# Scan by pairs of chunks, one root per group applied at the turn, taps spread over products, weights split before the seam

## The chip, the cores and the metric

The kernel runs on one core of a Trainium2 chip. The metric is device time in microseconds (us) from start to end of one launch. The kernel before takes 2141.73 us, the median of three runs (2140.22 to 2143.49).

The core has engines with a queue each, worked off in order: TensorE (PE, matrix products), VectorE (DVE), ScalarE (ACT, functions such as exp and silu, whose tables are loaded by an instruction ACT_TABLE_LOAD), GpSimd (POOL) and SyncE (SP), which issues most transfers (DMA). SBUF is the on-chip memory, PSUM the banks into which TensorE writes. Engines wait for each other by semaphores.

## The reference

One block of a streaming encoder on x of 1024 frames by 1024 channels, float32. Cut to what the change touches:

```python
proj = rms_norm(x, norm1_g) @ w_in
lru_x, lru_gate, z, xbc, dt_raw, gates = _split(proj, IN_WIDTHS)
...
xbc = silu(causal_dw_conv(xbc, ssd_conv_w, ssd_conv_b))     # 4 taps
xs, Bm, Cm = _split(xbc, ...)                               # 2048, 512, 512 columns
# scan, per chunk and head:
a_cs = cumsum(dt * A)
decay = exp(where(causal, a_cs[l] - a_cs[s], -inf))
y_diag = (C B^T * decay) @ xdt
states = B^T (decay_to_end * xdt);  h = h * chunk_decay + states
y = y_diag + (C h_prev) * exp(a_cs) + D * xs
# gated norm per group of 512 columns:
y = y * silu(z)
yg = yg * rsqrt(mean(yg * yg) + EPS) * ssd_norm_g
...
merged = g_a * (y_a @ w_branch[:LRU]) + g_b * (y_b @ w_branch[LRU:])
h = x + merged @ w_out
h = h + swiglu(rms_norm(h, norm2_g))
```

There are 32 heads of 64 columns in 4 groups; y_a is the output of another branch, the LRU, a convolution and a linear recurrence.

## The kernel before, in words

Products of float32 matrices are made of two parts: a tile is split (split, L82 and L83) into a high part, cast by ScalarE, and a low part, src minus high, by VectorE; a product takes three matmuls (high by high, high by low, low by high).

The stages, by the time in which they run:

- 0 to 97 us: the first norm, then products of half the gate columns (g_first, g_second, L308). Beside them row_sums makes, in two halves of two row blocks, sums and differences of the normalised x (f00 to f11) and splits them into t1 to t4 (L386, L387).
- 90 to 455 us, the units: 20 units of 256 columns each, 12 for xbc and 8 for the gates. A unit is made of 7 products (5 for the gates) over quarter matrices, so that sums of quarters stand on one side (unit_sums, GpSimd) and t1 to t4 on the other; useq lists the products. unit_prepare splits a weight part (wc) three products ahead, unit_after takes results out. conv_rows makes the convolution of a finished xbc row block: ScalarE the last tap with the bias (L432), VectorE three taps (L435), ScalarE the silu (L437), SP the transfer.
- 455 to 463 us, the seam: t1 to t4 and the units' tiles are given back, the LRU's memory is taken, its first weight is split into w_hi and w_lo.
- 463 to about 682 us: the LRU branch (L659 on). The steps dt and the sums acs of the scan are made in it.
- about 695 to 1075 us, the scan: 4 groups of 8 chunks of 128 frames (the kernel's chunk has twice the reference's length). Per chunk gate_z makes the product of z (24 matmuls, L145) two chunks ahead and its silu sz. chunk_in loads acs, broadcast over 128 partitions, as ed (L733), GpSimd cuts it to the triangle (L735), ScalarE takes 8 exponentials with the bias -acs (L738), one per head; VectorE multiplies it with B C (L762). chunk_out makes the output of the state (py, L775), the new state's product (pst, L779) and the 8 products of ed (pd, L782). VectorE and GpSimd add and gate them (L798 to L803), ScalarE squares with a sum (L807). After every second chunk VectorE makes two columns of reciprocal roots in 12 operations (rsqrt_dve), ScalarE scales both y by them (L812) and SP writes y to memory.
- 1075 to about 1357 us: the branch products over w_branch. add_v reads y back, TensorE turns it (transpose), ScalarE and VectorE split it with the norm's gain. Four of the 16 tiles of y are read at the end of the scan.
- then the merge, w_out, the second norm and the feed-forward layer.

The order within an engine's queue is made by the framework's scheduler out of the code's order and the dependencies; it may put a later independent instruction ahead of a waiting one. A tile named with bufs=n has n buffers in turn. Weights are loaded ahead by load_next and split by split_next.

## Time and profile before

| | us |
|---|---|
| median of three runs | 2141.73 |
| the profiled execution, its own time | 2142.65 |
| its span (first to last instruction) | 2140.8 |
| TensorE busy | 2018.7 (94%) |
| VectorE busy | 1282.9 (60%) |
| ScalarE busy | 965.2 (45%) |
| GpSimd busy | 697.0 (33%) |

Times in the rows are counted from the span's start. The mean granted clock of TensorE is 0.967 of 2.4 GHz. In a row "idle before, releaser" is time in which the engine had nothing to do before the instruction, and what ended it; "issue" is a wait for nothing that the profile shows. An engine's busy time is not its work at full speed: a TensorE at half clock is busy twice as long for the same matmuls.

### The profile page before, as it was taken

To read this page: it belongs to the slowest core of one execution; us is meant where nothing else is said; L and a number is where in the kernel's file an instruction comes from. 1 tells how busy PE (TensorE), PEld (TensorE's weight loads), DVE (VectorE), ACT (ScalarE), POOL (GpSimd) and SP (SyncE) were. 2 spreads that over 40 slices of the span, in tenths; PEclk is the share of its full clock that TensorE was granted. 3 is DMA by queue.
4 is the path that set the end of the run, shared out by engine and by line. 5 is a ranking of instruction groups with operands and counts; after the bars stand their busy time and mean duration, and the time that the engine had idled before them with its cause. 6 is when DMAs were issued, how large, how long until landed. Compare 5 with 4: busy or idle time off the path is not lost.

```text
span 2140.8 us, 23980 instructions
## 1 busy us (share of the span) xinstructions
PE 2018.7 (94%) x8972; PEld 1636.9 (76%) x8972; DVE 1282.9 (60%) x1695; ACT 965.2 (45%) x1545; POOL 697.0 (33%) x472
## 2 busy tenths in 40 slices
PE   6899999989999998898799999998999999999998
PEld 4677777768787786777578788886888888888887
DVE  7887777755575566566624555558554545446445
ACT  5455455447777677677532211335232323242112
POOL 4644444410000667676500011016333233203000
PEclk9999999999999999999599999999999999999999
DMA  5443344332112543432333334531323222256212
GB/s 185 122 123 99 99 127 140 109 102 61 60 54 94 185 143 98 138 99 79 98 99 104 120 119 145 185 104 40 109 69 99 79 69 89 79 176 196 90 60 79
DMA packets 201560, 231.59 MB, mean 108 GB/s; under 512 B 11148, under 2 KB 154980, under 8 KB 201444
## 3 DMA queue, kind: packets, MB, share of 16 engines
q1 hardware_dynamic: 201444, 230.06, 33.7%
q8 instruction: 71, 1.16, 0.2%
q14 instruction: 45, 0.37, 0.1%
HBM read 174.32 MB, written 55.71 MB: 107 GB/s over the span
## 4 chain that ended last, share of the span: by engine, by line
PE 48%; DVE 1%; ACT 1%; issue 0%; ACTq 0%; DVEq 0%
PE mm L308 19%; PE mm L134 13%; PE mm L145 10%; PE aux L145 6%; PE turn L705 1%; PE aux L206 0%; DVE slot L1092 0%; ACT slot L1091 0%; DVE o L1256 0%; DVE xb L1077 0%; DVE xr L1061 0%; DVE t L1081 0%; DVE wc L83 0%; DVE rs_t L163 0%; DVE xb L1083 0%
## 5 line engine op out<-in xcount | busy, mean ns | idle before, releaser
L308 PE MATMUL mm<-slot,wc 128*128 128x512 f32 x2376 | 564.5, 396 | 14.8 <-DVE wc L83 8.2
L308 PEld LDWEIGHTS mm<-slot,wc 128*128 128x128 f32 x2376 | 447.7, 189 | 124.1 <-DVE wc L83 10.6
L134 PE MATMUL mm<-slot,w_hi 128*128 128x512 f32 x768 | 243.6, 398 | 8.7 <-ACT w_hi L82 8.7
L308 PE MATMUL mm<-t,wc 128*128 128x512 f32 x960 | 228.2, 394 | 11.8 <-ACT wc L82 7.1
L145 PE MATMUL mm<-wz,slot 128*128 128x512 f32 x768 | 208.2, 418 | 17.3 <-ACT sz L725 12.9
L308 PEld LDWEIGHTS mm<-t,wc 128*128 128x128 f32 x960 | 181.7, 190 | 53.4 <-ACT wc L82 14.6
L145 PE MATMUL mm<-slot,slot 128*128 128x512 f32 (+1 forms) x924 | 213.0, 387 | 0.0
L145 PEld LDWEIGHTS mm<-slot,slot 128*128 128x128 f32 x924 | 171.6, 188 | 35.0
L145 PEld LDWEIGHTS mm<-wz,slot 128*128 128x128 f32 x768 | 149.0, 200 | 53.6 <-ACT sz L725 16.6
L134 PEld LDWEIGHTS mm<-slot,w_hi 128*128 128x128 f32 x768 | 145.9, 190 | 43.6 <-ACT w_hi L82 9.2
L83 DVE TENSOR_TENSOR wc<-s,wc 128x512 fp32r<-128x512 f32 x168 | 156.1, 952 | 32.6 <-ACT wc L82 32.5
L134 PE MATMUL mm<-slot,w_lo 128*128 128x512 f32 x384 | 151.5, 396 | 0.0
L145 PE MATMUL aux<-slot,slot 128*128 128x512 f32 x528 | 124.4, 389 | 0.0
L435 DVE SCALAR_TENSOR_TENSOR conv<-rows,par,conv 128x1023 f32<-128x1023 f32 (+2 forms) x72 | 111.0, 1541 | 17.3 <-ACT conv L432 17.3
L145 PEld LDWEIGHTS aux<-slot,slot 128*128 128x128 f32 x528 | 99.1, 188 | 20.6
L1028 POOL TENSOR_TENSOR u_u<-u_u,e 128x512 f32<-128x512 f32 x22 | 28.7, 1305 | 261.6 <-DVE u_u L1022 261.6
L82 ACT CAST wc<-s 128x512 fp32r<-128x512 f32 x168 | 98.5, 618 | 16.6 <-DVE wc L83 7.7
L82 ACT CAST slot<-w_raw 128x1024 fp32r<-128x1024 f32 x42 | 43.9, 1051 | 129.4 <-PE mm L145 48.1
L82 ACT CAST w_hi<-w_raw 128x1024 fp32r<-128x1024 f32 x40 | 41.6, 1046 | 118.0 <-PE mm L134 107.2
L907 POOL TENSOR_TENSOR acc<-acc,gt 128x1024 f32<-128x1024 f32 x8 | 20.0, 2512 | 213.3 <-DMA gt<-g_dram 212.2
L134 PE MATMUL mm<-v_even,w_hi 128*128 128x512 f32 x256 | 84.4, 408 | 1.5 <-ACT w_hi L82 1.5
L83 DVE TENSOR_TENSOR slot<-w_raw,slot 128x1024 fp32r<-128x1024 f32 x42 | 53.6, 1281 | 53.4 <-ACT slot L82 53.3
(276 smaller groups left out, 3494.9 us busy)
## 6 DMA issues: line engine op xcount, KB each, us to landing
w_raw<-in_w_in_dram SPq DMA_DIRECT2D x60, 512.0 KB, 3.9
ed<-acs_dram SPq DMA_DIRECT2D x32, 512.0 KB, 3.6
xbc_dram<-conv SPq DMA_DIRECT2D x24, 512.0 KB, 2.7
w_raw<-in_w_branch_dram SPq DMA_DIRECT2D x24, 512.0 KB, 3.4
w_raw<-in_w_ffn_in_dram SPq DMA_DIRECT2D x22, 512.0 KB, 3.9
raw_pair<-in_w_ffn_in_dram SPq DMA_DIRECT2D x22, 512.0 KB, 4.1
act_dram<-act SPq DMA_DIRECT2D x22, 512.0 KB, 2.7
act_raw<-act_dram SPq DMA_DIRECT2D x22, 512.0 KB, 3.5
```

The source lines that it names most:

```text
L82: nc.scalar.copy(out=hi, in_=src)
L83: nc.vector.tensor_tensor(out=lo, in0=src, in1=f32(hi), op=ALU.subtract)
L134: nc.tensor.matmul(ps[:m, :], ww[:, k, :], xx(p, k, h), start=(k == 0 and i == 0), stop=(k == nk - 1 and i == 2))
L145: nc.tensor.matmul(ps, xx(p, k), ww(q, k), start=(k == 0 and i == 0), stop=(k == nk - 1 and i == 2))
L308: nc.tensor.matmul(ps, w[:, k, :], x[q][:, k, :], start=(start and k == 0 and i == 0), stop=(k == 3 and i == 2), skip_group_check=True)
L435: nc.vector.scalar_tensor_tensor(out=t[:, d:], in0=x[:, :S - d], scalar=tap[j], in1=t[:, d:], op0=ALU.mult, op1=ALU.add)
L705: nc.tensor.transpose(out=pt[:, i * P:(i + 1) * P], in_=raw[:, o:o + P], identity=ident)
L907: nc.gpsimd.tensor_tensor(out=acc[m], in0=acc[m], in1=gate_in(1, m), op=ALU.mult)
L1028: nc.gpsimd.tensor_tensor(out=d["u3"], in0=d["u3"], in1=d["e5"], op=ALU.add)
```

## The change

Four parts:

1. Row sums start one product earlier each, and t3 and t4 are split together at the end; the four tiles are taken in the reverse order.
2. conv_rows emits only its second tap at once; the third and the fourth with silu and transfer are put in a list, from which one is taken after each following product.
3. At the last unit product t1 to t4 are given back at once, and the next stage's first weight is split there in the pool of wz (w_early), a second one right after that unit.
4. In the scan ed is made by chunk_ed: load, a subtraction of acs on VectorE, the triangle cut with fill -1e4; the exponential is one of 128x1024. The code loads two chunks' ed and takes two silus and two exponentials one after the other. y is written to memory unscaled; the sums of squares stay in ss_g, and the roots of a group's 8 chunks are made in one go, on 8 columns, and kept in rs_all, by which add_v multiplies y when it is read back, ahead of the turn. ed has 3 buffers for 2, sz 4 for 3, xd 3 for 4, xs2 and xs3 1 for 2.

```diff
-    for name in ("t1", "t2", "t3", "t4"):
+    for name in ("t4", "t3", "t2", "t1"):
         xc[name] = [tq_pool.tile([P, 4, 512], F32R, name=f"{name}_{q}") for q in range(2)]
+
+    def row_parts(name, k, src):
+        ks = slice(k, k + 2)
+        hi = xc[name][0][:, ks]
+        nc.scalar.copy(out=hi, in_=src)
+        nc.vector.tensor_tensor(out=xc[name][1][:, ks], in0=src, in1=f32(hi), op=ALU.subtract)
...
-        for kh in range(2):
-            for h in range(2):
+        for h in range(2):
+            for kh in range(2):
                 f[kh, h] = ubuf(f"f{kh}{h}", [P, 2, 512])
                 (nc.vector if kh == 0 else nc.gpsimd).tensor_tensor(
                     out=f[kh, h], in0=f32(xq[0][kh][h][:, ks]), in1=f32(xq[1][kh][h][:, ks]), op=ALU.add)
         f11, f12, f21, f22 = f[0, 0], f[0, 1], f[1, 0], f[1, 1]
...
         nc.vector.tensor_tensor(out=f11, in0=f12, in1=f11, op=ALU.subtract)
-        parts("t1", f11)
+        row_parts("t1", k, f11)
         nc.gpsimd.tensor_tensor(out=f12, in0=f22, in1=f12, op=ALU.subtract)
         nc.vector.tensor_tensor(out=f22, in0=f22, in1=f11, op=ALU.subtract)
-        parts("t2", f22)
+        row_parts("t2", k, f22)
         nc.gpsimd.tensor_tensor(out=f21, in0=f21, in1=f22, op=ALU.subtract)
-        parts("t3", f12)
-        parts("t4", f21)
+        return f12, f21
...
         g_second(m - 1, gb_[m - 1])
-        if m == 4:
-            row_sums(0)
-        elif m == 6:
-            row_sums(2)
+        if m == 3:
+            t34_0 = row_sums(0)
+        elif m == 5:
+            t34_2 = row_sums(2)
+        elif m == 7:
+            row_parts("t3", 0, t34_0[0])
+            row_parts("t3", 2, t34_2[0])
+            row_parts("t4", 0, t34_0[1])
+            row_parts("t4", 2, t34_2[1])
...
-        for j in (2, 1, 0):
+
+        def one_tap(j):
             d = 3 - j
             nc.vector.scalar_tensor_tensor(out=t[:, d:], in0=x[:, :S - d], scalar=tap[j], in1=t[:, d:],
                                            op0=ALU.mult, op1=ALU.add)
-        nc.scalar.activation(out=t, in_=t, func=AF.Silu)
-        nc.sync.dma_start(out=xbc_dram[tile_no // 2][(tile_no % 2) * P:(tile_no % 2 + 1) * P, :], in_=t)
+
+        def last():
+            one_tap(0)
+            nc.scalar.activation(out=t, in_=t, func=AF.Silu)
+            nc.sync.dma_start(out=xbc_dram[tile_no // 2][(tile_no % 2) * P:(tile_no % 2 + 1) * P, :], in_=t)
+
+        one_tap(2)
+        later.extend([lambda: one_tap(1), last])
+
+    later = deque()
...
+    def w_early():
+
+        raw, _ = loaded.popleft()
+        t = keep_pool.tile([P, 2, KT, P], F32R, name="w_early", tag="wz", bufs=4)
+        split(t[:, 0], t[:, 1], raw)
+        ready.append((t[:, 0], t[:, 1]))
+        load_next()
...
         product(banks[n, HOME[p]], w[:, 0], w[:, 1], xc[XOF[p]], HOME[p] == p)
+        if later:
+            later.popleft()()
+        if i == len(useq) - 1:
+            while later:
+                later.popleft()()
+            t_stack.close()
+            keep_pool = keep_stack.enter_context(phase("keep_pool"))
+            w_early()
         unit_after(n, p)
-    t_stack.close()
+    w_early()
     u_stack.close()
...
-    nacs_t = const.tile([P, NC, NH], F32, name="nacs_t")
+    rs_all = const.tile([P, NG, NC], F32, name="rs_all")
     dec_t = const.tile([P, NC, NH], F32, name="dec_t")
     eacs_t = const.tile([P, NC, NH], F32, name="eacs_t")
     d_bc = const.tile([P, NH], F32, name="d_bc")
-
-    keep_stack = ExitStack()
-    keep_pool = keep_stack.enter_context(phase("keep_pool"))
     sel_last = keep_pool.tile([P, P], F32, name="sel_last")
...
-        nc.vector.tensor_scalar(out=nacs_t, in0=acs_t, scalar1=-1.0, scalar2=None, op0=ALU.mult)
...
+                by_chunk = raw.rearrange("p (c d) -> p c d", d=P)
+                nc.vector.tensor_tensor(out=by_chunk, in0=by_chunk, in1=bcast(rs_all[:, g], P), op=ALU.mult)
...
-            sz = pp.tile([P, GC], F32, name="sz", tag="sz", bufs=3)
+            return zp
+
+        def silu(zp):
+            sz = pp.tile([P, GC], F32, name="sz", tag="sz", bufs=4)
             nc.scalar.activation(out=sz, in_=zp, func=AF.Silu)
             return sz
...
-        def chunk_in(g, c, b_ch, c_ch, xs_ch):
+        def chunk_ed(g, c):
+            hs = slice(g * HG, (g + 1) * HG)
+            ed = pp.tile([P, HG, P], F32, name="ed", tag="ed", bufs=3)
+            nc.sync.dma_start(out=ed, in_=acs_dram[c, hs, :].unsqueeze(0).broadcast_to([P, HG, P]))
+            nc.vector.tensor_tensor(out=ed, in0=ed, in1=bcast(acs_t[:, c, hs], P), op=ALU.subtract)
+
+            nc.gpsimd.affine_select(out=ed, in_=ed, pattern=[[0, HG], [1, P]], compare_op=ALU.is_ge,
+                                    fill=-1.0e4, base=0, channel_multiplier=-1)
+            return ed
+
+        def chunk_in(g, c, b_ch, c_ch, xs_ch, ed):
             h0 = g * HG
             hs = slice(h0, h0 + HG)
             cs = slice(c * P, (c + 1) * P)
-            ed = pp.tile([P, HG, P], F32, name="ed", tag="ed", bufs=2)
-            nc.sync.dma_start(out=ed, in_=acs_dram[c, hs, :].unsqueeze(0).broadcast_to([P, HG, P]))
-
-            nc.gpsimd.affine_select(out=ed, in_=ed, pattern=[[0, HG], [1, P]], compare_op=ALU.is_ge,
-                                    fill=-1.0e30, base=0, channel_multiplier=-1)
-            for h in range(HG):
-                nc.scalar.activation(out=ed[:, h, :], in_=ed[:, h, :], func=AF.Exp, bias=nacs_t[:, c, h0 + h:h0 + h + 1])
             pt = bank()
             nc.tensor.matmul(pt[:, :P], b_ch[:, cs], c_ch[:, cs], start=True, stop=True)
             if c < NC - 1:
@@ -757,12 +793,12 @@
                 xw = pp.tile([P, 2, GC], F32R, name="xw", tag="xw", bufs=1)
                 nc.scalar.copy(out=xw[:, 0, :], in_=flat(xwf))
                 nc.gpsimd.tensor_tensor(out=xw[:, 1, :], in0=flat(xwf), in1=f32(xw[:, 0, :]), op=ALU.subtract)
-            xd = pp.tile([P, HG, 64], F32, name="xd", tag="xd", bufs=4)
+            xd = pp.tile([P, HG, 64], F32, name="xd", tag="xd", bufs=3)
             nc.vector.tensor_tensor(out=xd, in0=pxv, in1=bcast(d_bc[:, hs], 64), op=ALU.mult)
             nc.vector.tensor_tensor(out=ed, in0=ed, in1=pt[:, :P].unsqueeze(1).broadcast_to([P, HG, P]), op=ALU.mult)
             return ed, xdt, xw, xd, b_tm
...
+        ss_g = pp.tile([P, NG, NC], F32, name="ss_g")
...
             nc.gpsimd.tensor_tensor(out=yf, in0=yf, in1=sz, op=ALU.mult)
-            if not pend:
-                ss2[0] = pp.tile([P, 2], F32, name="ss2", tag="ss2", bufs=2)
-            n = len(pend)
-            nc.scalar.activation(out=sz, in_=yf, func=AF.Square, accum_out=ss2[0][:, n:n + 1])
-            pend.append((c, yf))
-            if n:
-                r = rsqrt_dve(pp, ss2[0], 1.0 / GC, 2)
-                for i, (cc, y) in enumerate(pend):
-                    nc.scalar.activation(out=y, in_=y, func=AF.Copy, scale=r[:, i:i + 1])
-                    nc.sync.dma_start(out=y_dram[g][:, :, cc * P:(cc + 1) * P], in_=y.rearrange("p (a b) -> p a b", b=P))
-                pend.clear()
+            nc.scalar.activation(out=sz, in_=yf, func=AF.Square, accum_out=ss_g[:, g, c:c + 1])
+            nc.sync.dma_start(out=y_dram[g][:, :, cs], in_=yf.rearrange("p (a b) -> p a b", b=P))
+            if c == NC - 1:
+                nc.vector.tensor_copy(out=rs_all[:, g, :], in_=rsqrt_dve(pp, ss_g[:, g, :], 1.0 / GC, NC))
             return state
...
+        xs_ch = [rows_of(i, f"xs{i}", 2 if i < 2 else 1) for i in range(4)]
...
-                szs += [gate_z(0, 0), gate_z(0, 1)]
+                eds = [chunk_ed(0, 0), chunk_ed(0, 1)]
+                for e in eds:
+                    nc.scalar.activation(out=e, in_=e, func=AF.Exp)
+                zs = [gate_z(0, 0), gate_z(0, 1)]
+                szs += [silu(z) for z in zs]
+                zs = []
             for c in range(NC):
-                parts = chunk_in(g, c, b_ch, c_ch, xs_ch)
-                if c + 2 < NC:
-                    szs.append(gate_z(g, c + 2))
-                elif g + 1 < NG:
+                parts = chunk_in(g, c, b_ch, c_ch, xs_ch, eds.pop(0))
+                ahead = (g, c + 2) if c + 2 < NC else (g + 1, c + 2 - NC)
+                if ahead[0] < NG:
                     if c + 2 == NC:
                         wz_next(4)
-                    szs.append(gate_z(g + 1, c + 2 - NC))
+                    zs.append(gate_z(*ahead))
+                if c % 2 and ahead[0] < NG:
+                    eds.append(chunk_ed(*ahead))
+                    szs += [silu(z) for z in zs]
+                    zs = []
+                    for e in eds:
+                        nc.scalar.activation(out=e, in_=e, func=AF.Exp)
                 state = chunk_out(g, c, c_hl, parts, state, szs.pop(0))
+                if c % 2 == 0 and ahead[0] < NG:
+                    eds.append(chunk_ed(*ahead))
                 if g == NG - 1 and c >= NC - 2:
                     wz_next(2)
...
-                        xs_next = ([] if c == 3 else xs_next) + [rows_of(4 * g + 1 + c, f"xs{c - 3}", 2)]
+                        xs_next = ([] if c == 3 else xs_next) + [rows_of(4 * g + 1 + c, f"xs{c - 3}", 2 if c < 5 else 1)]
```

In the scheduled program the units have the same instructions in the same order on all engines as before, from the first wc of VectorE on. At the front, VectorE has the low part of the gate weight g_lo for m = 3 behind the first sums, and the second half's part of t2 ahead of the first wc, where it stood behind it. GpSimd's work in the scan is the same.

**ScalarE at the seam.** Before; the first row is the sigmoid of the last gate unit's first rows, neg_a belongs to the scan's steps:

```order
L343 ACTIVATE rows_3240<-rows_3240,par_135 128x512
L475 ACTIVATE rows_3241<-rows_3241,par_135 128x1024
L578 ACT_TABLE_LOAD
L578 ACTIVATE neg_a<-prm 32x1
L82 CAST w_hi<-w_raw 128x1024 x2
L192 ACTIVATE scr<-scr 128x8
```

and now:

```order
L343 ACTIVATE rows_3236<-rows_3236,par_135 128x512
L82 CAST w_early<-w_raw 128x1024 x2
L488 ACTIVATE rows_3237<-rows_3237,par_135 128x1024
L607 ACT_TABLE_LOAD
L607 ACTIVATE neg_a<-prm 32x1
L82 CAST w_hi<-w_raw 128x1024
L561 ACTIVATE u<-mm,par_135 128x512
```

The casts of the first two weights (w_early is called twice) stand ahead of the second sigmoid, in tiles of their own; the weights after them are cast one by one.

**ScalarE in the scan,** two chunks in the middle of the first group, before:

```order
L807 ACTIVATE sz,ss_5354<-xd 128x512
L725 ACT_TABLE_LOAD
L725 ACTIVATE sz<-mm 128x512
L738 ACT_TABLE_LOAD
L738 ACTIVATE ed<-ed,nacs_t 128x128 x8
L812 ACTIVATE xd<-xd,rs_r 128x512 x2
L793 CAST state_hl<-state 128x512
L807 ACTIVATE sz,ss_5577<-xd 128x512
L725 ACT_TABLE_LOAD
L725 ACTIVATE sz<-mm 128x512
L738 ACT_TABLE_LOAD
L738 ACTIVATE ed<-ed,nacs_t 128x128 x8
```

and now (L758 is the silu, L879 the exponential, L840 the square):

```order
L840 ACTIVATE sz,ss_g<-xd 128x512
L758 ACT_TABLE_LOAD
L758 ACTIVATE sz<-mm 128x512
L879 ACT_TABLE_LOAD
L879 ACTIVATE ed<-ed 128x1024
L829 CAST state_hl<-state 128x512
L840 ACTIVATE sz,ss_g<-xd 128x512
L758 ACT_TABLE_LOAD
L758 ACTIVATE sz<-mm 128x512
L879 ACT_TABLE_LOAD
L879 ACTIVATE ed<-ed 128x1024
```

The scaling of two y is gone and the exponential is one instruction; silu and exponential take turns as before, each with its table load, so that there are 28 + 27 + 1 loads (silus, exponentials, the first exponentials) in the scan's lines where there were 25 + 25.

**VectorE in the scan,** a chunk before, with the root of two chunks behind it (of its nine Newton operations, three times the same three, the first three are shown):

```order
L801 TENSOR_TENSOR xd<-aux,xd 128x512
L791 TENSOR_TENSOR state<-aux,state 128x512
L752 TENSOR_TENSOR xdt<-turn,dt_t 128x512
L761 TENSOR_TENSOR xd<-turn,d_bc 128x512
L211 TENSOR_TENSOR b_tm<-aux,b_tm 128x128
L762 TENSOR_TENSOR ed<-ed,aux 128x1024
L170 TENSOR_SCALAR rs_v<-ss_5354 128x2
L172 TENSOR_SCALAR rs_i<-rs_v 128x2
L174 TENSOR_SCALAR rs_r<-rs_i 128x2
L163 TENSOR_TENSOR rs_t<-rs_r 128x2
L164 SCALAR_TENSOR_TENSOR rs_t<-rs_t,rs_v 128x2
L165 SCALAR_TENSOR_TENSOR rs_r<-rs_t,rs_r 128x2
```

and a chunk now:

```order
L827 TENSOR_TENSOR state<-aux,state 128x512
L837 TENSOR_TENSOR xd<-aux,xd 128x512
L788 TENSOR_TENSOR xdt<-turn,dt_t 128x512
L797 TENSOR_TENSOR xd<-turn,d_bc 128x512
L211 TENSOR_TENSOR b_tm<-aux,b_tm 128x128
L798 TENSOR_TENSOR ed<-ed,aux 128x1024
L765 TENSOR_TENSOR ed<-ed,acs_t 128x1024
L834 TENSOR_TENSOR yo<-aux,eacs_t 128x512
```

The root is gone from here. The subtraction (L765), for the chunk three further on, stands last, ahead of the next chunk's yo (L834).

## Rows read from the trace of the kernel before

**Rows 1.** busy time by stretch: us, then PE, PEld, DVE, ACT, POOL, PEclk, DMA share, GB/s

```profile
722.00:1004.50 282.50, 253.81 (x1297) 208.27 (x1296) 188.05 (x325) 203.76 (x420) 194.71 (x156) 0.94 0.36 116
1004.50:1075.00 70.50, 48.82 (x188) 37.98 (x185) 43.30 (x89) 43.38 (x94) 41.87 (x36) 0.57 0.29 90
1075.00:1460.00 385.00, 384.04 (x1726) 311.88 (x1726) 189.88 (x248) 107.61 (x154) 35.48 (x22) 0.99 0.38 125
```

**Rows 2.** TensorE's waits, 60 to 490 us: total us, times, longest

```profile
PE mm L134 <- ACT w_hi L82: 8.7, 1, 8.7
PE mm L308 <- DVE wc L83: 8.2, 5, 6.7
...
PE mm L308 <- DVE rows L455: 4.8, 2, 3.4
```

**Rows 3.** TensorE's waits in the scan, 722 to 1075 us

```profile
PE mm L145 <- ACT sz L725: 12.9, 11, 2.4
PE aux L775 <- ACT state_hl L793: 9.5, 8, 2.8
```

**Rows 4.** line L801: count, duration ns min/median/max, first and last start in us

```profile
L801 DVE TENSOR_TENSOR xd<-aux,xd x32: 676/684/693, 716.9 to 1063.9; 128x512 f32<-128x512 f32 x32
```

**Rows 5.** VectorE's timeline, chunk 24 of the scan: start, us, instruction, idle before

```profile
985.65 0.69 DVE L801 TENSOR_TENSOR xd<-aux,xd 128x512 f32<-128x512 f32 x1
```

**Rows 6.** busy time, 59 to 97 us, columns as in rows 1

```profile
59.00:97.00 38.00, 27.77 (x106) 21.71 (x105) 38.00 (x20) 15.98 (x23) 29.19 (x12) 0.87 0.42 125
```

**Rows 7.** VectorE's timeline at the end of that stretch

```profile
86.95 2.82 DVE L83 TENSOR_TENSOR wc<-w_raw,wc 128x512 fp32r<-128x512 f32 x1
89.70 4.53 DVE L387 TENSOR_TENSOR t<-f,t 128x1024 fp32r<-128x1024 f32 x2
```

**Rows 8.** ScalarE's timeline at the seam: start, us, instruction, idle before

```profile
453.26 0.72 ACT L343 ACTIVATE rows<-rows,par 128x512 f32<-128x512 f32 x1
455.48 1.15 ACT L475 ACTIVATE rows<-rows,par 128x1024 f32<-128x1024 f32 x1 [1.49 <-DVE rows L470]
...
462.29 1.99 ACT L82 CAST w_hi<-w_raw 128x1024 fp32r<-128x1024 f32 x2 [4.14 <-issue]
```

**Rows 9.** TensorE's clock behind the seam, columns as in rows 1

```profile
463.40:468.20 4.80, 4.80 (x11) 3.78 (x12) 3.07 (x7) 3.97 (x6) 1.90 (x2) 0.50 0.16 36
```

**Rows 10.** groups on ScalarE, 722 to 1075 us: xcount, busy us, mean ns, idle before

```profile
L738 ACT ACTIVATE ed<-ed,nacs_t 128x128 f32<-128x128 f32 x240 | 73.8, 389 | 10.1 <-POOL ed L735 9.8
...
L738 ACT ACT_TABLE_LOAD x24 | 30.8, 1283 | 0.4
L812 ACT ACTIVATE xd<-xd,rs_r 128x512 f32<-128x512 f32 x32 | 21.3, 713 | 19.0 <-DVE rs_r L165 19.0
```

**Rows 11.** groups on VectorE, 722 to 1075 us

```profile
L762 DVE TENSOR_TENSOR ed<-ed,aux 128x1024 f32<-128x1024 f32 x30 | 36.3, 1208 | 0.3 <-PE aux L740 0.3
...
L165 DVE SCALAR_TENSOR_TENSOR rs_r<-rs_t,rs_r 128x2 f32<-128x2 f32 x48 | 19.0, 396 | 1.4
L83 DVE TENSOR_TENSOR wz<-w_raw,wz 128x1024 fp32r<-128x1024 f32 x12 | 18.0, 1498 | 5.2 <-ACT wz L82 5.2
...
L174 DVE TENSOR_SCALAR rs_r<-rs_i 128x2 int32<-128x2 int32 x16 | 6.8, 427 | 0.4
```

**Rows 12.** tile ed, landing of its 32 transfers

```profile
DMA to landing us min/median/max: 3.3/3.6/9.7
```

**Rows 13.** VectorE's timeline, a root of two chunks in the last group

```profile
1048.11 0.55 DVE L170 TENSOR_SCALAR rs_v<-ss 128x2 f32<-128x2 f32 x1 [2.15 <-ACT sz L807]
...
1051.52 1.26 DVE L165 SCALAR_TENSOR_TENSOR rs_r<-rs_t,rs_r 128x2 f32<-128x2 f32 x1
...
1053.79 0.16 DVE L165 SCALAR_TENSOR_TENSOR rs_r<-rs_t,rs_r 128x2 f32<-128x2 f32 x1
```

**Rows 14.** GpSimd's timeline at the same time

```profile
1051.50 1.26 POOL L800 TENSOR_TENSOR xd<-xd,yo 128x512 f32<-128x512 f32 x1 [1.63 <-DVE rs_t L164]
```

**Rows 15.** ScalarE's timeline at the end of the scan

```profile
1074.06 1.99 ACT L82 CAST w_hi<-w_raw 128x1024 fp32r<-128x1024 f32 x2 [2.37 <-issue]
```

More of the change, by code (lines that the diff above doesn't have):

```diff
@@ L382, in row_sums @@
         f11, f12, f21, f22 = f[0, 0], f[0, 1], f[1, 0], f[1, 1]
-        def parts(name, src):
-            hi = xc[name][0][:, ks]
-            nc.scalar.copy(out=hi, in_=src)
-            nc.vector.tensor_tensor(out=xc[name][1][:, ks], in0=src, in1=f32(hi), op=ALU.subtract)
         nc.vector.tensor_tensor(out=f11, in0=f12, in1=f11, op=ALU.subtract)
-        parts("t1", f11)
+        row_parts("t1", k, f11)
         nc.gpsimd.tensor_tensor(out=f12, in0=f22, in1=f12, op=ALU.subtract)
         nc.vector.tensor_tensor(out=f22, in0=f22, in1=f11, op=ALU.subtract)
-        parts("t2", f22)
+        row_parts("t2", k, f22)
         nc.gpsimd.tensor_tensor(out=f21, in0=f21, in1=f22, op=ALU.subtract)
-        parts("t3", f12)
-        parts("t4", f21)
+        return f12, f21
     for m in range(3, KT):
@@ L512, in hybrid_block_kernel @@
     g_second(KT - 1, gb_[KT - 1])
+    keep_stack = ExitStack()
+    def w_early():
[4 more added lines that the diff above has]
+        load_next()
     for i, (n, p) in enumerate(useq):
@@ L763, in chunk_in @@
             return ed, xdt, xw, xd, b_tm
-        pend, ss2 = [], [None]
+        ss_g = pp.tile([P, NG, NC], F32, name="ss_g")
         def chunk_out(g, c, c_hl, parts, state, sz):
@@ L823, in hybrid_block_kernel @@
         b_ch, c_ch = rows_of(16, "b_ch", 2, keep_pool), rows_of(20, "c_ch", 2)
-        xs_ch = [rows_of(i, f"xs{i}", 2) for i in range(4)]
+        xs_ch = [rows_of(i, f"xs{i}", 2 if i < 2 else 1) for i in range(4)]
         szs = []
```

## The prediction

> **What bounds the kernel now.** I read the busy time of each engine by stages first, then TensorE's waits in the stages that the change touches, then the other engines there. From 1075 us on TensorE computes without a break (384.04 of 385 us) [rows 1]; what other engines do there can cost only if it grows past their reserve. In the scan it is otherwise. From 722 to 1004.5 us TensorE is busy 253.81 of 282.5 us at a mean clock of 0.94, so 28.7 us are waiting and 253.81 x 0.06 = 15 us are lost to the clock [rows 1]. From 1004.5 to 1075 us, where the gate products have run out, it is busy 48.82 of 70.5 us at 0.57, and no other engine reaches 44 us: that stretch hangs on a chain through all engines. TensorE's waits in the scan are many short ones, for the silu that frees a bank and for the state that ScalarE casts [rows 3]. Before the scan there are two large holes: 8.7 us at the seam, for w_hi from ScalarE, and 6.7 us at the end of the first products, for a weight part wc from VectorE; the waits for rows inside the units are 4.8 us in all [rows 2].
>
> The rhythm of the scan is read from the add of pd (L801), of which there is one per chunk: 32 of them from 716.9 to 1063.9 us, and that of chunk 24, the first of the last group, at 985.65 [rows 4, 5]. So the 24 intervals before it are (985.65 - 716.9) / 24 = 11.2 us, the last 7 are (1063.9 - 985.65) / 7 = 11.18. TensorE's own work per chunk at full clock is 253.81 x 0.94 / (282.5 / 11.2) = 9.46 us. The two rhythms are the same although the second has almost no gates: neither is TensorE's pace.
>
> **Taps in the units: 0.** ScalarE, VectorE and GpSimd get the same instructions in the same order there as before; the scheduler had spread the taps already. I expect the waits for rows in [rows 2] again. Bounds -2 to +2, for the order can't differ but the start can.
>
> **Row sums: +3 us.** Between 59 and 97 us VectorE has no gap. In its new order a part of t2 goes ahead of the first wc, which took 2.82 us, and a g_lo moves behind the first sums [rows 6, 7]. TensorE waits 6.7 us for just that wc [rows 2], and one part of t more in front of it, 2.27 us (4.53 for the two in [rows 7]), makes it late by as much; a g_lo that comes late makes its product late as well. A gain is possible too, since the sums start earlier: bounds -2 to +6. I take 3, nearest to the one part.
>
> **The seam: -10.5 us.** The last unit product ends at 454.6. The first sigmoid ends at 453.98, the second runs 455.48 to 456.63, then a table is loaded, and w_hi starts only at 462.29 after 4.14 us in which nothing that the trace shows holds it [rows 8]: the program makes it wait for the transfer that reads the last gate rows out of that memory. Now both early casts stand between the two sigmoids, in memory of t1 to t3, and wait for the raw weights and TensorE alone: 1.99 us for both from about 454 us, VectorE's first part at about 455.5. TensorE then starts at about 455.2 in place of 463.4: 8.2 us. After the hole the chip also granted 0.5 of TensorE's clock, its level of 1.2 GHz, from 463.4 to 468.2 [rows 9]; 4.8 us at half are 2.4 at full clock. Together 10.6; I take 10.5. The second sigmoid gets later by 2 us, and behind it stand only the steps of the next stage, where TensorE has its own next weights. Bounds -12 if nothing else waits, -6 if the raw weights of the next products come late, because two more loads pass the others in SP's queue.
>
> **The scan: -40 us.** What goes, from the stretch 722 to 1075:
> - ScalarE: 240 exponentials of 128x128 take 73.8 us, 2.46 per chunk; one of 128x1024, like the second sigmoid, takes 1.15 [rows 8, 10]. That saves 1.3 per chunk. The scaling of y (32 x 0.713, and 19.0 us of waiting before it) goes [rows 10].
> - VectorE: 16 chains of 12 operations on 2 columns, six lines from 19.0 us (L165) to 6.8 (L174), 77.8 in all [rows 11]. Four chains on 8 columns stay: 4/16 of it, 19 us.
> - Waits: y leaves straight after the gate's product, no longer after square, chain and scale.
>
> What comes:
> - 32 subtractions of 128x1024. No row has this very form: an operation of that size with a PSUM operand takes 1.208, a split with both inputs in SBUF 1.498 [rows 11]. I take 1.5, nearest in kind; 32 x 1.5 = 48 us, bounds 39 (1.208) and 79 (1.208 and a whole GpSimd operation of 1.26 in front).
> - It waits for its transfer at the queue's head on VectorE; behind it stand yo, state and the add of pd. The transfer lands after 3.6 us, in the median, 9.7 at most [rows 12]. It is issued when pd of the chunk is through, so the subtraction ends about 5.5 us after that pd, the select (about 1.1) at 6.6 and the exponential, in ScalarE's queue behind square, load, silu and load, at about 9.2.
> - Table loads: the title says shared, but the new order on ScalarE has silu and exponential in turns in every chunk, as before. 28 + 27 + 1 = 56 loads stand against 50: 6 x 1.283 = 7.7 us more [rows 10]. The pairs in the code share no load.
> - TensorE does the same work, GpSimd too.
>
> By this schedule ScalarE's loop closes at 9.2 us after the previous pd, plus 0.65 for the casts of wz and c_hl as a mean (15 casts of about 1.04 over 24 chunks): 9.85; TensorE's pace is 9.46. Engines in order, with clocks that fall after each wait, don't reach such a pace: I add 0.4 and take 10.25. Gain in 24 intervals: 24 x 0.95 = 22.8. In the last 7 there is little to hide behind: the chain on the two columns took VectorE from 1048.11 to 1053.95, with the add of pd behind it and ScalarE's scale behind that, 5.8 us per pair [rows 13], 2.9 per chunk of which I count 2.5: 7 x 2.5 = 17.5. Together 40. Bounds: -15 if the subtraction eats the steady part, -66 at TensorE's pace.
>
> **Into the branch products: -4 us.** The last add of pd starts at 1063.9, w_hi at 1074.06 [rows 4, 15], since it waited for the last y. Now y leaves 2.2 us after that add and lands some 2.7 later; but in VectorE's order w_lo stands behind the last chain on 8 columns and a multiplication by rs_all, at about 8.3 against 11.3. I take -4; bounds -6 to +2.
>
> **Branch products: +1 us.** 12 of the 16 multiplications by the root fall here, about 1.3 each, on a VectorE that is 189.88 of 385 us busy [rows 1]. TensorE covers them; without that cover 16 us. I take 1, bounds 0 to 4.
>
> **The sum.** 2142.65 (the profiled execution: span 2140.8 and 1.85 around it; 0.9 above the median) + 3 - 10.5 - 40 - 4 + 1 = 2092.
>
> **A rule against the change.** While GpSimd runs its add from 1051.50 for 1.26 us, VectorE's operation on two columns that starts at 1051.52 takes 1.26 as well and ends with it, the last of its kind 0.16 [rows 13, 14]. So an operation of VectorE with two inputs in SBUF stands still while GpSimd works. The Trainium skill, page "SBUF — State Buffer", section "SBUF: two separate sides", states it as a lock on a shared pair of ports, exclusive for a whole instruction, for VectorE operations with two SBUF inputs. The rows agree. The old bias of the exponential took no part in that; the new subtraction does.
>
> **Rivals.**
> 1. The subtraction and GpSimd shut each other out. GpSimd is busy 194.71 of 282.5 us [rows 1], 69% of the time, so a subtraction waits 0.69 x 0.63 (half an operation) = 0.43 on the mean, and the select, gate product or xw behind it up to 1.21 for the subtraction. Both stand in the row that ends in the exponential: some 0.9 more per chunk, 11.15, which leaves nothing of the steady gain, and 14 of the end: 2142.65 + 3 - 10.5 - 1 - 14 - 4 + 1 = 2117. For it: 1.498 in place of 1.208 [rows 11]. Against: the chains that go were shut out in the same way.
> 2. The scan comes down to TensorE's 9.46: 24 x 1.74 + 7 x 3.4 = 66 in place of 40: 2066. For it: the operations that go lie in the loop. Against: 56 loads, and two rhythms near each other.
> 3. Slower: the subtraction at VectorE's head waits for a late transfer. yo is wanted about 1 us after the subtraction ends; what the landing exceeds 4.6 by is added to each chunk. To be slower in all, the chunk must reach 11.7, which is a landing of 4.6 + 1.45 = 6.1 us. At 7: 12.65, 31 x 1.45 = 45 more: 2142.65 + 45 - 10.5 = 2177. For: 9.7 is seen. Against: the median of 3.6 with the same bytes.
> 4. The scan keeps its 11.2, held by something not removed: 2142.65 + 3 - 10.5 = 2135.
>
> **Chances and range.** Forecast 0.58 (2080 to 2104), rival 1 0.20, rival 2 0.12, rival 3 0.05, rival 4 0.05. The range 2064 to 2126 takes in the first two rivals. Within 0.2% (4.3 us, about what a measurement here can tell from none) is only an edge of rivals 3 and 4: 0.02; slower 0.05; faster 0.93.
>
> **What would show it.** Right: the hole before L134 under 1.5 us and no half clock behind it; 56 table loads in the scan; adds of pd some 10.25 apart, then 8.7; no scale on ScalarE; the waits of the units unchanged; the wait for the first wc up from 6.7 to near 9. Wrong: subtractions of 2 us and more (rival 1), VectorE idle before the subtraction for its transfer (rival 3), or intervals of 11.2 (rival 4).

## The result, and the profile after

The changed kernel takes 2078.95 us, the median of four runs (2073.72 to 2081.05), against 2142.61 for the kernel before in its four: the ratio is 0.9701, with a 95% interval of 0.9681 to 0.9721. The forecast was 2092, the range 2064 to 2126. The profiled execution took 2073.72 us (span 2072.0), 68.9 less than that of before; it is the fastest of the four, so its pieces add up to some 5 us more than the medians. The ratios of the experiments leave out two slow runs of the kernel before, of 3322.46 and 7699.24 us.

Busy time of the changed kernel between the adds of pd of chunks 0, 24 and 31, columns as in rows 1:

```profile
702.17:946.11 243.94, 233.23 (x1280) 197.02 (x1280) 180.89 (x239) 161.42 (x224) 203.70 (x152) 0.99 0.42 138
946.11:1015.36 69.25, 54.00 (x232) 44.15 (x230) 46.68 (x61) 31.40 (x52) 52.90 (x42) 0.65 0.28 85
```

and of the kernel before between the same adds:

```profile
716.95:985.65 268.70, 241.26 (x1243) 198.01 (x1242) 178.63 (x309) 195.83 (x403) 188.95 (x150) 0.94 0.37 119
985.65:1063.91 78.26, 62.33 (x254) 50.17 (x255) 51.70 (x95) 48.23 (x107) 51.41 (x44) 0.66 0.26 84
```

In the first stretch TensorE is now busy 233.23 of 243.94 us at 0.99, where it had 241.26 of 268.70 at 0.94: it bounds the scan there, nearly. In the second, TensorE's share (54.00 of 69.25 us against 62.33 of 78.26) and its clock (0.65 against 0.66) are much like before. The adds of pd themselves, the changed kernel's line L837, as in rows 4 and 5:

```profile
L837 DVE TENSOR_TENSOR xd<-aux,xd x32: 676/690/693, 702.2 to 1015.4; 128x512 f32<-128x512 f32 x32
```

```profile
946.11 0.68 DVE L837 TENSOR_TENSOR xd<-aux,xd 128x512 f32<-128x512 f32 x1
```

The 24 intervals are (946.11 - 702.17) / 24 = 10.16 us, the last 7 are (1015.36 - 946.11) / 7 = 9.89; the prediction had 10.25 and 8.7, before they were 11.2 and 11.18.

TensorE's waits from 60 to 490 us, as in rows 2:

```profile
PE mm L308 <- ACT wc L82: 8.6, 6, 2.6
PE mm L308 <- DVE rows L468: 7.4, 2, 3.7
PE mm L308 <- DVE g_lo L83: 5.3, 2, 3.4
...
PE mm L134 <- ACT w_early L82: 1.1, 1, 1.1
PE mm L308 <- DVE wc L83: 0.8, 2, 0.4
```

The hole of 8.7 at the seam is 1.1 now, the 6.7 for the first wc is gone, and waits for g_lo have come. The waits for rows are 7.4 where they were 4.8 [rows 2]. That is partly a matter of names, since the five longer holes inside the units stand at the same places in both kernels and are put down now to wc, now to rows; added up they grew from 11.3 to 14.3 us. ScalarE's timeline at the seam, as in rows 8, and TensorE's clock behind it, as in rows 9:

```profile
449.64 0.72 ACT L343 ACTIVATE rows<-rows,par 128x512 f32<-128x512 f32 x1
451.04 1.99 ACT L82 CAST w_early<-w_raw 128x1024 fp32r<-128x1024 f32 x2 [0.67 <-PE mm L308]
452.94 1.15 ACT L488 ACTIVATE rows<-rows,par 128x1024 f32<-128x1024 f32 x1
```

```profile
452.14:457.00 4.86, 4.86 (x21) 3.89 (x22) 2.72 (x5) 3.43 (x4) 0.00 (x0) 1.00 0.76 226
```

The two casts run between the sigmoids, 11 us earlier than w_hi did [rows 8], and the clock stays at 1.00 where it was 0.50.

By stretches the 68.9 us of the two profiled executions fall so (first matmuls and adds of each stage, in us from the span's start):

| stretch | before | after | difference |
|---|---|---|---|
| start to the first product of t1 | 96.61 | 95.42 | -1.2 |
| units | 357.7 | 355.2 | -2.5 |
| last unit matmul to first LRU matmul | 9.1 | 1.5 | -7.6 |
| LRU branch to the first gate of z | 209.6 | 203.8 | -5.9 |
| to the first add of pd | 43.9 | 46.3 | +2.3 |
| 24 intervals of the scan | 268.7 | 243.9 | -24.8 |
| last 7 intervals | 78.3 | 69.3 | -9.0 |
| to the first branch matmul | 11.3 | 7.3 | -4.0 |
| branch products to the end | 1065.7 | 1049.4 | -16.3 |

The 2.5 of the units is not the change but the clock of this one execution: b1_nosub and b2_root, below, have the same order there and take 357.7 and 361.0 (see the last section). The scan has 56 table loads, as forecast.

The last line is the surprise. From the middle of the branch products on, all engines have the same instructions in the same order in both kernels. Yet TensorE does them faster. The same 300 us in the feed-forward layer, all of it busy at a granted clock of 1.00, before:

```profile
1500.00:1800.00 300.00, 300.00 (x1292) 243.22 (x1291) 153.46 (x204) 91.61 (x167) 108.63 (x80) 1.00 0.27 84
```

and after:

```profile
1500.00:1800.00 300.00, 300.00 (x1325) 248.43 (x1324) 158.86 (x206) 96.05 (x175) 107.88 (x78) 1.00 0.28 85
```

1292 recorded matmuls against 1325, 2.6% more. From start to start they take 232.4 ns before and 226.7 after, and the LRU branch, the branch products and those matmuls of the units that stream a slot show the same kind of difference.

### The profile page after: what moved, and what is told of

Same layout as the page of the kernel before. It is cut to its first block, busy times and chain, and to the rows that moved or that the text cites. A ratio compares the mean times of both kernels' runs of the same rounds, so it can differ in the third digit from the quotient of the medians.

```text
span 2072.0 us, 23647 instructions
## 1 busy us (share of the span) xinstructions
PE 1975.9 (95%) x8972; PEld 1624.4 (78%) x8972; DVE 1298.3 (63%) x1602; ACT 910.7 (44%) x1295; POOL 718.0 (35%) x472
## 4 chain that ended last, share of the span: by engine, by line
PE 67%; DVE 6%; ACT 4%; POOL 3%; issue 2%; DMA 2%; POOLq 0%; DVEq 0%; ACTq 0%
PE mm L308 24%; PE mm L134 18%; PE mm L145 15%; PE aux L145 6%; PE aux L818 2%; DVE conv L440 1%; DMA v_raw<-y_dram 1%; DMA w_raw<-in_w_in_dram 1%; PE aux L672 1%; PE turn L735 1%; POOL xw L795 1%; PE aux L815 1%; POOL xd L839 1%; DVE slot L1133 1%; POOL state_hl L830 1%
## 5 line engine op out<-in xcount | busy, mean ns | idle before, releaser
L308 PE MATMUL mm<-slot,wc 128*128 128x512 f32 x2376 | 549.9, 391 | 7.3 <-DVE slot L1133 5.2
L308 PE MATMUL mm<-t,wc 128*128 128x512 f32 x960 | 226.9, 392 | 16.1 <-ACT wc L82 8.6
L134 PE MATMUL mm<-slot,w_hi 128*128 128x512 f32 x704 | 218.0, 390 | 0.0
L145 PE MATMUL mm<-wz,slot 128*128 128x512 f32 x768 | 196.8, 401 | 4.6 <-ACT sz L758 1.9
L145 PEld LDWEIGHTS mm<-wz,slot 128*128 128x128 f32 x768 | 141.5, 190 | 34.9 <-ACT wz L82 2.7
L134 PEld LDWEIGHTS mm<-slot,w_hi 128*128 128x128 f32 x704 | 132.0, 188 | 27.8 <-DVE dt_rows L612 0.3
L134 PE MATMUL mm<-slot,w_lo 128*128 128x512 f32 x352 | 137.1, 389 | 0.0
L674 POOL TENSOR_TENSOR gi<-gi,u 128x1024 f32<-128x1024 f32 x8 | 20.0, 2505 | 186.4 <-ACT gi L673 186.4
```

Of the source, the lines that this page charges most:

```text
L134: nc.tensor.matmul(ps[:m, :], ww[:, k, :], xx(p, k, h), start=(k == 0 and i == 0), stop=(k == nk - 1 and i == 2))
L145: nc.tensor.matmul(ps, xx(p, k), ww(q, k), start=(k == 0 and i == 0), stop=(k == nk - 1 and i == 2))
L308: nc.tensor.matmul(ps, w[:, k, :], x[q][:, k, :], start=(start and k == 0 and i == 0), stop=(k == 3 and i == 2), skip_group_check=True)
```

## The experiments

Times are medians, ratios against runs of the kernel before on the same chip.

The scheduler orders each program anew. By the built programs the padded kernels keep the order of the kernel that they are made from, and b2_root nearly keeps that of the changed kernel on ScalarE and GpSimd. In b1_nosub, b3_bias, b4_pair, d1_yo and d3_both the scan has another order on every engine, in a4_front its last group has. From the last add of pd to the first branch matmul these six take 9.7 to 10.9 us, where the changed kernel and b2_root take 7.3. Their times are those of edit and order together.

**Where a tile begins.** The change takes a table of 1024 bytes per partition (nacs_t) out of the constant pool and puts one of 128 (rs_all) in. By the addresses in the built programs most tiles of the pools behind it, the slots among them, move by 896 bytes (those of the scan and wz, which parts 3 and 4 rearrange, by other distances); the weights (w_hi, wc), in pools at the other end of SBUF, do not. The tiles that these matmuls stream as moving operand (slot) begin at 608 before and 736 after, by the remainder to 1024; the weights at 992.

```diff
# a1_pad: the changed kernel, 896 bytes
+    pad_t = const.tile([P, 224], F32, name="pad_t")
+    nc.gpsimd.memset(pad_t[:, 0:1], 0.0)
# a2_pad: the kernel before, [P, 32]; c1_pad128: the changed kernel, [P, 32]; c2_pad32: the changed kernel, [P, 8]
```

> The changed kernel with an unused tile of 896 bytes per partition in the constant pool, so that everything behind it in SBUF lies where it lay before the change (a table of 1024 bytes had gone and one of 128 had come). In the profiles the same matmuls of the feed-forward layer follow each other every 226.7 ns after the change and every 232.4 before it, at the same granted clock. Theory A (the place in SBUF decides it): the pace falls back to about 232 ns from the units to the feed-forward layer; 2079 + about 16 to 20 = 2095 to 2099 us. Theory B (the state of the chip in one run decides it): no change, 2079 us within 4, and the pace has nothing to do with the padding.

> The kernel before with an unused tile of 128 bytes per partition in the constant pool, which gives all behind it the same remainder by 1024 bytes as after the change. Theory A, if only the remainder counts: the feed-forward layer's matmuls come every 226.7 ns, about 2142 - 20 = 2122 us. Theory A, if the distance itself counts: nothing certain. Theory B: 2142 us and 232 ns as before.

> The changed kernel with 128 unused bytes in the constant pool. The tiles that the fast matmuls read as moving operand (slot) begin at 736 bytes, by the remainder to 1024, after the change, at 608 before it and in the run with 896 bytes; the weights and the tiles t lie at 992 in all. Here the slots begin at 864. If the remainder to 256 decides (736 and 992 give 224, 608 and 864 give 96): slow again, 232 ns in the feed-forward layer and some 2097 us. If 608 itself is the bad place: 226.7 ns and 2079.

> The changed kernel with 32 unused bytes in the constant pool: the slots begin at 768, a multiple of 256. If what counts is that moving operand and weights have the same remainder to 256 (224), this is off by 32 and slower than 226.7 ns. If a place in the slot's own 256 bytes is bad (96) and others are good: 226.7 ns or less and 2079 us or less.

| kernel | slots begin at, mod 1024 (mod 256) | pace in the feed-forward layer, ns | time, us | ratio (95%) |
|---|---|---|---|---|
| before | 608 (96) | 232.4 | 2142.6 | 1 |
| after | 736 (224) | 226.7 | 2078.95 | 0.9701 (0.9681 to 0.9721) |
| a1_pad | 608 (96) | 232.4 | 2096.83 | 0.9786 (0.9770 to 0.9801) |
| a2_pad | 736 (224) | 226.7 | 2123.32 | 0.9906 (0.9890 to 0.9922) |
| c1_pad128 | 864 (96) | 232.4 | 2097.15 | 0.9788 (0.9774 to 0.9803) |
| c2_pad32 | 768 (0) | 233.3 | 2102.65 | 0.9810 (0.9796 to 0.9825) |

The 300 us of a1_pad, c1_pad128 and c2_pad32, in this order:

```profile
1500.00:1800.00 300.00, 300.00 (x1292) 243.24 (x1291) 153.08 (x202) 92.35 (x169) 103.29 (x75) 1.00 0.25 79
```

```profile
1500.00:1800.00 300.00, 300.00 (x1293) 243.26 (x1292) 150.90 (x202) 92.59 (x169) 102.91 (x75) 1.00 0.25 79
```

```profile
1500.00:1800.00 300.00, 300.00 (x1288) 240.98 (x1287) 150.38 (x201) 92.42 (x169) 104.54 (x77) 1.00 0.24 79
```

Theory A holds and B does not: an unused tile costs the changed kernel its 18 us again, and 128 unused bytes make the kernel before 20 us faster with nothing else changed. The remainder to 256 orders all six: 224 is fast, 96 and 0 are slow. 224 is also that of the weights.

Whether the two must agree, or 224 is good by itself, can be read from matmuls that take their weights from other places. In the products with w_out both operands are slots, so their remainders are alike in every kernel. 35 us of the branch products (slot with w_hi and w_lo), then 35 us of those with w_out, in the kernel before (remainders 96 and 224, then 96 and 96):

```profile
1300.00:1335.00 35.00, 35.00 (x152) 28.38 (x151) 13.42 (x17) 4.91 (x5) 0.00 (x0) 1.00 0.32 97
1358.00:1393.00 35.00, 35.00 (x156) 28.95 (x155) 13.51 (x25) 6.83 (x11) 0.00 (x0) 1.00 0.60 226
```

The same 35 us in c2_pad32 (0 and 224, then 0 and 0) also have 152 and 156 matmuls, in the changed kernel (224 throughout) 157 and 156. With w_out all three kernels are equally fast, 226.7 to 226.9 ns from start to start. In c2_pad32 a slot also streams fast against w_early (0 and 0, 227 ns in the median) and slowly against w_hi (0 and 224, 234 ns), in the same stage on the same line. In the changed kernel one tile of the branch products, v_odd, lies at 32 and keeps a slow pace against w_hi (232 ns in the median, v_even at 224 has 227). So 96 and 0 are not bad places, and 224 is not needed: in these products the pairs that agree in the remainder to 256 are fast and the others slow. No run moved the weights alone.

**The seam alone,** on the kernel before:

```diff
+            t_stack.close()
+            keep_pool = keep_stack.enter_context(phase("keep_pool"))
+            w_early()
         unit_after(n, p)
+    w_early()
```

> The kernel before with the seam alone: the four tiles t taken in reverse order, and two early weight splits at the last unit product. The prediction's term was -10.5; the traces show the hole 8.73 against 1.13 and no half clock behind it, so 7.6 + 2.4 = 10: about 2132 us. Rival: if the faster pace of the later stages came with this edit, about 2112. If the seam's gain is given back in the LRU stage: 2142.

2146.55 us, ratio 1.0017 (1.0007 to 1.0027): slower. The hole is 1.13 us, the first gate of z comes at 664.86 in place of 673.00, and the first add of pd 8.2 us earlier. All of it is lost in the scan:

```profile
L813 DVE TENSOR_TENSOR xd<-aux,xd x32: 677/684/692, 708.8 to 1066.2; 128x512 f32<-128x512 f32 x32
```

357.4 us from first to last against 347.0 [rows 4]. No line of the scan was edited, but its scheduled order is another from the second group on, on all engines (silus, selects and casts stand elsewhere). So the seam's gain is real, about 8 us, and a scan in another order took 10 more. That this order does it is read from the two programs; no run put the old order behind the new seam.

**Row sums and taps** as before, in the changed kernel:

> The changed kernel with the row sums and the convolution taps written as before. The prediction said +3 for the row sums and 0 for the taps, so 2079 - 3 = 2076 us. By the traces the first product of t1 came 1.2 us earlier in the changed kernel, so 2079 + 1 = 2080. Rival: the taps spread over products are what made the units' matmuls follow each other faster (229 to 227 ns, 3.8 us): 2084.

2084.32 us, 0.9726 (0.9706 to 0.9745): 5.4 more than the changed kernel, the intervals just overlapping. The first product of t1 comes at 96.88, 1.5 us later; the two waits for rows are 3.74 and 3.75 us with the old form of the taps, 3.72 and 3.73 with the new one, and the pace in the units is 227 ns with either. The taps do nothing that can be seen, as forecast; the row sums gain a little where a loss was forecast. The time is the 2084 of the rival, but its reason is not there: what is left of the 5.4 us lies in parts that were not edited, the scan (318.6 us from first to last add, 313.2 in the changed kernel) and the way from it to the branch products (10.9 against 7.3).

**The subtraction** taken out:

```diff
-            nc.vector.tensor_tensor(out=ed, in0=ed, in1=bcast(acs_t[:, c, hs], P), op=ALU.subtract)
```

> The changed kernel without the 32 subtractions of acs (they are left out, the rest stays). Rival 1 of the prediction (subtraction and GpSimd shut each other out, in the row that ends in the exponential): each interval loses up to 0.9 us, 31 x 0.9 = 28, 2051 us. The forecast's reading (hidden behind ScalarE's loop, which is some 9.85 with or without it): only what the queue behind it on VectorE waits, at most 0.2 per chunk, 2073 to 2079 us.

The kernel so made leaves out a step of the calculation and is run for its time alone: 2078.94 us, 0.9698 (0.9684 to 0.9713), in sum nothing. In the changed kernel the subtraction is held by GpSimd, as rival 1 said. VectorE and GpSimd at the same time:

```profile
705.70 2.07 DVE L765 TENSOR_TENSOR ed<-ed,acs_t 128x1024 f32<-128x1024 f32 x1 [0.23 <-DMA ed<-acs_dram]
...
716.81 2.06 DVE L765 TENSOR_TENSOR ed<-ed,acs_t 128x1024 f32<-128x1024 f32 x1
```

```profile
705.64 1.04 POOL L826 TENSOR_TENSOR state<-state,dec_t 128x512 f32<-128x512 f32 x1
...
715.76 2.03 POOL L792 TENSOR_TENSOR xwf<-xdt,dte_t 128x512 f32<-128x512 f32 x1
```

Both subtractions run beside an operation of GpSimd and take 2.07 and 2.06 where 1.21 is the least of the 32; the mean is 1.647. The sum of nothing has parts, though. By the profiles the 24 intervals are 238.7 us without the subtraction and 243.9 with it, 0.22 less each; the last 7 are 71.9 against 69.3, and the way to the branch products is 9.7 against 7.3. So the subtraction may cost up to 0.2 us per chunk in the steady part; since the order of the scan is another too, what each of the two does is not shown.

**The roots** after every second chunk again:

```diff
-            if c == NC - 1:
-                nc.vector.tensor_copy(out=rs_all[:, g, :], in_=rsqrt_dve(pp, ss_g[:, g, :], 1.0 / GC, NC))
+            if c % 2:
+                nc.vector.tensor_copy(out=rs_all[:, g, c - 1:c + 1], in_=rsqrt_dve(pp, ss_g[:, g, c - 1:c + 1], 1.0 / GC, 2))
```

> The changed kernel with the roots made after every second chunk again, 16 chains on 2 columns in place of 4 on 8; y still leaves unscaled. The prediction counted 2.5 us per chunk at the end for chain and scale together: if the chain alone does it, +15, 2094 us. If it was the scaling of y and its transfer that the loop waited for, the chain alone costs 0 to 5: 2079 to 2084.

2100.97 us, 0.9805 (0.9788 to 0.9821): 22 more. From first to last add of pd:

```profile
L837 DVE TENSOR_TENSOR xd<-aux,xd x32: 677/684/693, 706.4 to 1045.5; 128x512 f32<-128x512 f32 x32
```

339.1 us against 313.2, 0.84 per interval, in the 24 (263.7 against 243.9) as in the last 7 (75.4 against 69.3). The profiled execution is the slowest of its four and that of the changed kernel the fastest, so the 25.9 us here are more than the 22 of the medians. The chain alone does it, without the scaling.

**The bias** in eight exponentials again, in place of the subtraction:

```diff
-            nc.vector.tensor_tensor(out=ed, in0=ed, in1=bcast(acs_t[:, c, hs], P), op=ALU.subtract)
...
-                        nc.scalar.activation(out=e, in_=e, func=AF.Exp)
+            for h in range(HG):
+                nc.scalar.activation(out=ed[:, h, :], in_=ed[:, h, :], func=AF.Exp, bias=nacs_t[:, c, g * HG + h:g * HG + h + 1])
```

> The changed kernel with the eight exponentials of 128x128 with a bias again, and no subtraction (the table of -acs is back, so that the place of all else in SBUF has the same remainder by 1024 as after the change). ScalarE gets 1.3 us per chunk more, VectorE 1.5 to 1.7 less. If ScalarE's loop sets the rhythm, as the prediction has it: 24 x 1.0 = 24 more, 2103 us. If the subtraction and GpSimd hold each other as long as the eight pieces took (rival 1): 2079 within 5, or less.

2093.93 us, 0.9774 (0.9759 to 0.9789): 15 more, 0.41 per interval (326.0 us in all), between the two forecasts. The eight pieces are dearer than one with a subtraction, by about a third of the 1.3 us that they take more on ScalarE on the mean: 0.24 per interval in the 24 (249.6 us), 1.0 in the last 7 (76.5).

**Shared table loads,** forced by one exponential for two chunks:

```diff
-            ed = pp.tile([P, HG, P], F32, name="ed", tag="ed", bufs=3)
+            if c % 2 == 0:
+                ed_pair[0] = pp.tile([P, 2, HG, P], F32, name="ed", tag="ed", bufs=2)
+            ed = ed_pair[0][:, c % 2]
...
-                    for e in eds:
-                        nc.scalar.activation(out=e, in_=e, func=AF.Exp)
+                    pair_exp()
```

> The changed kernel with the ed of two chunks in one tile of two buffers and one exponential of 128x2048 for both, so that a table load is shared whatever the scheduler does: 98 loads in the program in place of 124, 33 us less on ScalarE. If ScalarE's loop sets the rhythm: intervals from 10.16 down to TensorE's 9.46, 24 x 0.7 = 17 less, 2062 us. If the waits are elsewhere: 2079. Against: an exponential of two chunks ends about 1 us later than one.

2089.03 us, 0.9750 (0.9736 to 0.9765): 10 more, with 26 loads fewer. ScalarE's waits in its scan:

```profile
ACT ed L765 <- POOL ed L775: 32.9, 12, 3.8
ACT state_hl L837 <- DVE state L835: 21.8, 10, 3.7
```

and in the changed kernel's:

```profile
ACT ed L879 <- POOL ed L767: 15.0, 15, 2.8
...
ACT state_hl L829 <- DVE state L827: 7.0, 4, 4.7
```

The common exponential waits for the second chunk's select, 32.9 us against 15.0, and the casts of the state stand behind it in the queue. What the fewer loads saved is not seen: the new waits, and the new order with them, cost more.

**GpSimd relieved.** In the changed kernel it is the busiest after TensorE in the 24 intervals, 203.70 us.

```diff
# d1_yo
-                nc.gpsimd.tensor_tensor(out=xd, in0=xd, in1=yo, op=ALU.add)
+                nc.vector.tensor_tensor(out=xd, in0=xd, in1=yo, op=ALU.add)
# d3_both: that, and
-                nc.gpsimd.tensor_tensor(out=parts[:, 1, :], in0=flat(new), in1=f32(parts[:, 0, :]), op=ALU.subtract)
+                nc.vector.tensor_tensor(out=parts[:, 1, :], in0=flat(new), in1=f32(parts[:, 0, :]), op=ALU.subtract)
```

> The changed kernel with the addition of yo to xd on VectorE in place of GpSimd, which is the busiest engine after TensorE in the scan (203.7 of 243.9 us in the 24 intervals, 52.9 of 69.25 in the last 7). GpSimd loses 1.28 per chunk, VectorE gets 0.7 with both inputs in SBUF, and two changes of engine go. If GpSimd's queue sets the end of the scan: the last 7 from 9.9 to about 8.6 each, 9 less, 2070 us; in the 24 intervals TensorE's 9.6 leaves at most 0.5 each. If VectorE is held by GpSimd in turn: 2079.

> As d1_yo, and the low part of the state on VectorE too: GpSimd loses 1.4 more per chunk, VectorE gets 0.7, in the chain from one state to the next. If GpSimd sets the rhythm: 2065 us. If VectorE becomes the one in the way (227 of 313 us are taken now): above the run with yo alone.

2074.42 us, 0.9679 (0.9665 to 0.9694), and 2072.13, 0.9670 (0.9653 to 0.9686): 4.5 and 7 less than the changed kernel. The intervals still overlap, so a gain over it is likely but not clear of noise. The second one's scan is 6.5 us shorter from first to last add:

```profile
L837 DVE TENSOR_TENSOR xd<-aux,xd x32: 676/684/693, 705.0 to 1011.7; 128x512 f32<-128x512 f32 x32
```

```profile
704.96:945.85 240.89, 232.85 (x1282) 197.47 (x1282) 206.81 (x280) 160.57 (x222) 141.63 (x109) 0.99 0.43 140
945.85:1011.70 65.85, 51.36 (x220) 41.06 (x219) 53.19 (x74) 33.98 (x53) 34.69 (x28) 0.68 0.27 84
```

GpSimd is down to 141.63 us, VectorE up to 206.81, TensorE busy 232.85 of 240.89. 3.0 of the 6.5 us go again on the way to the branch products (10.3 against 7.3). This is the lowest median of the kernels run. The end, 9.4 us per chunk, is still a chain: the 8.6 that were expected did not come.

## Why the prediction was right, and where it was wrong

The direction and the size came out, but the size partly by an effect that the prediction did not have. With the old remainder the changed kernel takes 2096.83 and 2097.15 (a1_pad, c1_pad128): the four edits themselves are worth 45.6 us, against 50.5 forecast, and the place of the tiles 18. That 45.6 is so near to 50.5 is in part luck: the row sums came out 4.5 us better than forecast, the end of the scan 8.5 worse.

- Taps, 0: right. The order was the same. The five holes of the units did not stay as they were, 14.3 us for 11.3, but they are 14.4 with the old taps (a4_front) and also in the kernel before with 128 bytes of padding (a2_pad), 11.5 in a1_pad: they go with the place of the tiles.
- Row sums, +3: wrong in sign. The failed step is "one part of t more in front of it, 2.27 us (4.53 for the two in [rows 7]), makes it late by as much". It took the wait of 6.7 us for wc as fixed and added to it. The first wc did end later, by 1.6 us (91.35 against 89.77). But the sums start earlier (the first of VectorE's at 38.90 in place of 41.48 us), and gate products that wait for g_lo now fill the place ahead of the first wc. The holes before t1, 10.2 us in all, became 7.9; the runs give -1.5 there.
- The seam, -10.5: right. 7.6 of the hole, and in the run with the seam alone the LRU branch is 2.6 shorter (207.0 against 209.6), the half clock's part; the other 3.3 of the 5.9 in the table are the place of the tiles (206.3 in a2_pad). What the prediction left out is that a gain ahead of a scheduled stage may change that stage's order: alone, the edit lost all of it.
- The scan, -40: too large. 33.8 came, of which some 4 belong to the place of the tiles (317.3 us from first to last add in a1_pad, 313.2 without its padding). The 24 intervals (-22.8 forecast, -24.8) came out nearly as worked out, 10.16 for 10.25, and 10.34 with the old place of the tiles (248.2 us in a1_pad). The 0.4 added to them for clocks that fall is shown by no run; the clock was 0.99 there. The end did not come out: -17.5 forecast, -9.0. There the chain on two columns was counted almost in full; b2_root shows it worth 0.87 per interval, not 2.5. That another chain, over GpSimd's adds and the state's parts, stands right behind it is what d3_both suggests, where these two moved and the end fell from 9.9 to 9.4; no run takes that chain apart.
- The reason given for the 10.25, ScalarE's loop, is only partly right. Less work for ScalarE by way of the loads makes the kernel slower (b4_pair); eight pieces for one cost a third of their time (b3_bias). What the scan lost most by was the chain on VectorE (b2_root, 22 us).
- Rival 1 described its mechanism rightly, subtractions of 2 us beside GpSimd (2.07 and 2.06 above, 1.647 on the mean), and priced it too high: without them the 24 intervals are 0.22 shorter each, not 0.9, and the total is the same (b1_nosub). The Trainium skill's rule of an exclusive lock, on the page "SBUF — State Buffer", section "SBUF: two separate sides", agrees with these two; it says nothing of whether the wait is on the path of a kernel.
- Into the branch products, -4: right, 7.3 us from the last add against 11.3.
- The end, +1: the 12 multiplications cost nothing that can be seen, but -16.3 came from the pace of TensorE (in a1_pad, with the multiplications and the old place, the stretch is 1065.2 us against 1065.7 before). The step that failed is one that was not made: the diff removes a table from the first pool in SBUF, and the prediction asked what that did to instructions, not to the addresses of everything behind it.

## What to carry to other kernels

When a stretch with the same instructions in the same order has another length after a change, compare the distance between like matmuls and then the addresses of both their operands; try an unused tile of some tens of bytes in the first pool before explaining the rest. An edit ahead of a stage that a scheduler orders, or inside it, has to be measured together with the order that it gives that stage. Work taken off an engine pays by the queue behind it: 16 chains of tiny operations in place of 4 cost 22 us, while taking out 32 subtractions of 1.65 us left the total as it was.

## What the runs showed of the hardware

The pace of matmuls of 128x512 float32 (their operands of the type fp32r) at full granted clock depends on where streamed operand and weights begin in SBUF. With the weights at a remainder of 224 to 256 it is 226.7 ns with the streamed operand at 224, 232.4 at 96 (with two addresses), 233.3 at 0; with both at 96 or both at 0 it is again 226.7 to 226.9. Over the kernel that is 18 to 24 us of 2079 (a1_pad, c2_pad32), about twice what the seam gave.

After holes of 3.73 and 3.94 us that end at 409 us, with the same order, TensorE's granted clock was 1.00 in the changed kernel's profile and 0.83 in that of b1_nosub (mean of 400 to 420 us, with a part at the lower of its two levels, 1.2 GHz); the drop cost the units 2.5 us there (their last matmul starts at 450.61 and 453.12). A hole of 3.75 at the same place in a4_front was followed by a drop too. Four runs of the changed kernel differ by 7.
